# Delta-rule layer: the triangular inverse's blocks turned on chip by VectorE instead of through DRAM, with other fill rates

## The chip, the cores and the metric

One core of one Trainium2 chip runs the whole kernel. The time is the device time of one execution in microseconds (us). The core's engines are named as in the profile: PE (matmuls), PEld (its weight loads), DVE (VectorE), ACT (ScalarE), POOL (GpSimd), and SP, which issues most DMAs.

## The reference

The kernel computes one layer on 512 latent tokens of width 1024 with 256 context tokens: a half-step SwiGLU block, then a neighbourhood attention and a gated delta rule side by side, merged by sigmoid gates, then a second half-step SwiGLU block. The part that matters here is the gated delta rule. It has 4 heads of size 128 and runs in two directions over chunks of tokens. For each chunk with keys k, queries q, decays g and weights beta it needs

```
B  = strict_lower(k k^T) * beta * exp(g_i - g_j)     (a gram matrix with decay)
T  = (I + B)^-1                                      (unit lower triangular)
A  = lower(q k^T) * exp(g_i - g_j)
u  = T (beta (v - exp(g) k S));  out = exp(g) q S + A u;  S <- exp(g_last) S + k_tail^T u
```

(B is meant up to transposition; the kernel keeps Bt, At and Tt.) In parallel the projections of the attention and the gates, products of the modulated tokens with the matrix w_in, have to be made as well.

## The kernel before

The layer runs stage by stage: modulation vectors, the first SwiGLU block, the projections, the delta rule, attention, merge, the second SwiGLU block. Matmuls in full precision are made of three: each operand is split into a high part (ACT casts `wh`, L137) and the rest (DVE subtracts `wl`, L139), and `mm3k` issues hi·hi (L192), lo·hi (L193) and hi·lo (L194), 128x512 each.

**The delta rule** has 48 systems of 128x128: six chunk positions s, two pairs of heads p, and for each of these two directions by two heads. They go in three batches of two positions (bi 0, 1, 2; st 0, 1 inside a batch), 16 systems each; `gram(p, s, ...)` makes one group of four. It loads the decay differences by a DMA from `gcd` into Dt (for some positions into an accumulator buffer, `oacc`, that is still free), masks them with four VectorE steps (L1122), takes the exponential on ACT, gets k·kT from PE and multiplies it by beta and the decay into Bt (four steps, L1128). For later positions it also makes At (L1134) from q·kT. The masks of positions 2 and 3 are issued behind the last Bt of the first batch, those of 4 and 5 behind an At.

**The inverse.** Each 128x128 matrix is inverted by its 32x32 diagonal blocks first. A batch has 64 of them, and `base_inverse` (L1140) works on all at once: each block lies on two partitions of the 128, with 16 of its columns on each. To get that layout, `gram` writes Bt to a DRAM buffer `bd` (L1131), and four DMAs read the diagonal blocks back, two of them by way of `Ltr` and an ACT copy of 64x1024 (L1153). POOL clears the start Xt and writes ones and, into L, a diagonal of -1 (L1155). Then 31 rows follow, one multiplication (L1159) and one reduction (L1160) each on DVE. The result goes to a second DRAM buffer, `rd` (L1163), from which `inverse` (L1173) loads T0 and T1 in four DMAs (L1180), turns both by 32x32 blocks on DVE (L1182, L1183) and goes on with products of 32x32, then 64x64 blocks on PE (`pi`), with DVE and ACT between them. It ends with Tt, which the scan steps of the positions (`scan_step`, PE tiles `pc`) take.

**Fills.** Between these dependent steps PE makes the 28 projections of the list FILLS, each in four steps of six matmuls; ACT or DVE moves each finished one (`spill`) to DRAM. `turn(kind, i)` emits fill steps at rates by a table: "g" in the grams of each batch, "l" ahead of the first inverse, "i" after each product of an inverse of batch i, "s" in the scan steps. They are issued behind the last matmul of the delta rule by `issue_after`. Fill steps come in one sequence, so each follows the one before it. What is left, but for the last three projections, is emitted before the attention begins; its first matmul writes the scores, `sc` (L1446).

**Order.** The code runs grams of batch 0, grams of batch 1, the turn "l", inverse (0,0), four steps of base 1, inverse (0,1), then scans and grams of batch 2 mixed with the inverses of batch 1, then inverse (2,0), two scans, inverse (2,1) and the last scans. A scheduler at build time places the instructions of each engine in one fixed order, by readiness and by the `issue_after` marks.

Of the kernel before, what the change touches and what calls it, by code (L numbers as in the profile page):

```python
# [13 lines left out]
ALU = mybir.AluOpType  # L14
AX = mybir.AxisListType.X
# [3 lines left out]
P = 128  # L19
# [12 lines left out]
MSTR = P * P + P  # L32
# [26 lines left out]
def body(ctx, tc, I, out, dbg=None):  # L59
# [983 lines left out]
    RATE = {"g": (2, 3.0, 0.7), "l": (7.2,), "i": (1.5, 0, 0), "s": (0.7, 0.9, 0.5)}  # L1043
# [63 lines left out]
    def decay_place(s, p):  # L1107

        if s == 2 or s < 2 and p == 1:
            a = 2 * (s == 2)  # L1110
            return oaccs[p if s == 2 else s][:, a:a + 2].rearrange("p a b c -> p (a b) c")
        return tl(gb_, [P, 4, P], "Dt", 2)[:]

    def gram(p, s, bd, g):
# [4 lines left out]
        for m, (d, c, i) in enumerate(mats):  # L1119
            msk = cst[:, (C_MF if d == 0 else C_MB):][:, 0:P]  # L1120
            with tc.issue_after(marks["At" if s > 3 else "Bt"]) if s > 1 else nullcontext():
# [3 lines left out]
        for n, t in enumerate(products(p, s)):  # L1125
            if n == 0:
                for m, (d, c, i) in enumerate(mats):
                    b = V.scalar_tensor_tensor(Bt[:, m], t[m] if s == 1 else t[:, m], beta[:, d, s, 2 * p + i:2 * p + i + 1], Dt[:, m], op0=ALU.mult, op1=ALU.mult)  # L1128
                if s < 2:
                    marks["Bt"] = b.ins  # L1130
                nc.sync.dma_start(bass.AP(bd.tensor, bd.offset + g * MSTR, [[P, P], [4 * MSTR, 4], [1, P]]), Bt[:])  # L1131
# [8 lines left out]
    def base_inverse(bd, rd):  # L1140


        L = tl(gb_, [P, 32, 32], "L")
        tr = tl(gb_, [64, 32, 32], "Ltr")
        Xt = tl(gb_, [P, 16, 32], "Xt", 2)
        G.memset(Xt[:], 0.0)
        for q in range(4):
            G.memset(Xt[32 * q:32 * q + 32].rearrange("p c k -> p (c k)")[:, q % 2:512:34], 1.0)
        st = 32 * P + 32
        for q in range(4):  # L1150
            dst = tr[32 * q:32 * q + 32] if q < 2 else L[32 * q:32 * q + 32]
            nc.sync.dma_start(dst, bass.AP(bd.tensor, bd.offset + (q // 2) * 8 * MSTR, [[st, 32], [P, 32], [1, 32]]))
        S.copy(L[0:64].rearrange("p r c -> p c r"), tr[:])  # L1153

        G.memset(L[:].rearrange("p r c -> p (r c)")[:, 0:1024:33], -1.0)  # L1155
        for i in range(1, 32):
# [3 lines left out]
            V.tensor_reduce(Xt[:, 0:c, i], t[:, 0:c, 0:i + 1], AX, ALU.add, negate=True)  # L1160
            if i % 4 == 0:
                yield
        nc.sync.dma_start(bass.AP(rd.tensor, rd.offset, [[512, P], [1, 512]]), Xt[:].rearrange("p c k -> p (c k)"))  # L1163
# [9 lines left out]
    def inverse(bi, st, rd, Bts):  # L1173


# [742 lines left out]
```

## Time and profile before

| | us |
|---|---|
| three runs | 1496.15, 1498.07, 1498.37 (median 1498.07) |
| the profiled execution | 1495.44 |
| its span in the profile | 1493.7 |
| mean granted TensorE clock | 0.993 |
| delta-rule stage around the change | from about 740 to 967 of the span |

In the profile's rows a time is in microseconds from the start of the span; a group's row gives line, engine, operation, destination<-sources and shapes, then busy time, mean ns of one instruction, and the idle time of the engine just before them with what ended it. A row of the waits gives who waited, for what, the total us, how many times, and the longest. A row of a stretch gives its bounds, its length, the busy us and count of each engine, then the granted clock and the DMA share with GB/s.

### The profile page before, as it was taken

The numbers are of one execution on the slowest core, as the hardware profiler recorded it, in microseconds if no ns is written. First come the engines' busy times: TensorE is split into PE (matmuls) and PEld (weight loads), VectorE is DVE, ScalarE is ACT, GpSimd is POOL, SyncE is SP. The second block draws the span as 40 slices with busy tenths as digits, with TensorE's granted clock in tenths as the row PEclk, the third lists the DMA queues.
The fourth block names the chain that finished last, engine by engine and source line by source line (L and its number), as shares of the span: only waits on it lengthen the run. The fifth ranks groups of instructions, "written<-read, shape, count | busy, mean of one in ns | idle before, by whom it ended". The sixth has DMA issues, their size and how long they took to land.

```text
span 1493.7 us, 23926 instructions
## 1 busy us (share of the span) xinstructions
PE 1434.0 (96%) x9117; PEld 1258.3 (84%) x9117; DVE 1144.7 (77%) x1975; ACT 661.9 (44%) x1090; POOL 212.4 (14%) x262
## 2 busy tenths in 40 slices
PE   6999999999999999999998899999999999999997
PEld 4778989999998777888886778877778999998886
DVE  8787869999987565768787886666668799886627
ACT  5433524434333286545544434376526454444310
POOL 1000000000000121223301002243321022220001
PEclk9999999999999999999999999999999999999999
DMA  9676665454559554222577524274344143234732
GB/s 372 211 257 225 222 238 187 137 174 166 170 198 404 181 178 129 84 92 88 159 222 203 167 68 125 92 276 131 100 169 149 64 129 113 85 114 134 263 98 84
DMA packets 109236, 248.56 MB, mean 166 GB/s; under 512 B 29049, under 2 KB 44481, under 8 KB 109121
## 3 DMA queue, kind: packets, MB, share of 16 engines
q1 hardware_dynamic: 104480, 229.40, 46.6%
q0 software_dynamic: 3056, 12.33, 2.2%
q10 hardware_dynamic: 1586, 5.32, 0.9%
q8 instruction: 71, 1.16, 0.3%
q14 instruction: 43, 0.35, 0.1%
HBM read 215.50 MB, written 31.50 MB: 165 GB/s over the span
## 4 chain that ended last, share of the span: by engine, by line
PE 71%; DMA 10%; DVE 9%; ACT 4%; issue 3%; POOL 1%; SPq 1%; DVEq 0%; ACTq 0%; POOLq 0%
PE ps L211 15%; PE pm L192 5%; PE pm L193 5%; PE pm L194 5%; PE ps L533 4%; PE ps L535 4%; PE ps L534 4%; PE ps L1692 3%; PE ps L1694 3%; PE ps L1693 3%; PE ps L193 3%; PE ps L192 3%; PE ps L194 3%; PE pc L1049 3%; DMA wr<-in_up_dram 2%
## 5 line engine op out<-in xcount | busy, mean ns | idle before, releaser
L139 DVE TENSOR_TENSOR wl<-wr,wh 128x1024 fp32r<-128x1024 f32 (+1 forms) x184 | 226.0, 1233 | 112.9 <-ACT wh L137 111.3
L137 ACT CAST wh<-wr 128x1024 fp32r<-128x1024 f32 (+1 forms) x184 | 185.6, 1013 | 278.5 <-PE pm L193 72.7
L192 PE MATMUL pm<-uxh,wh 128*128 128x512 f32 x320 | 131.6, 411 | 0.0
L194 PE MATMUL pm<-uxh,wl 128*128 128x512 f32 x320 | 126.3, 395 | 0.8 <-DVE wl L139 0.8
L193 PE MATMUL pm<-uxl,wh 128*128 128x512 f32 x320 | 126.5, 395 | 0.0
L211 PE MATMUL ps<-wh,hx 128*128 128x512 f32 x352 | 96.1, 391 | 0.1
L211 PEld LDWEIGHTS ps<-wh,hx 128*128 128x128 f32 x352 | 65.9, 188 | 14.5 <-ACT wh L137 0.5
L280 DVE SCALAR_TENSOR_TENSOR adap<-wr,crow 128x1024 f32<-128x1024 f32 x61 | 74.3, 1218 | 2.4 <-DMA wr<-in_w_adaT_dram 1.7
L192 PE MATMUL ps<-uh,wh 128*128 128x256 f32 (+1 forms) x208 | 69.2, 334 | 3.8 <-ACT wh L137 3.8
L194 PEld LDWEIGHTS pm<-uxh,wl 128*128 128x128 f32 x320 | 60.6, 190 | 13.8 <-DVE wl L139 0.9
L192 PEld LDWEIGHTS pm<-uxh,wh 128*128 128x128 f32 x320 | 60.8, 190 | 11.1 <-ACT spill L796 0.2
L193 PEld LDWEIGHTS pm<-uxl,wh 128*128 128x128 f32 x320 | 60.9, 190 | 10.3
L114 POOL TENSOR_TENSOR rs<-ve,mhalf 128x1 f32<-128x1 f32 (+2 forms) x46 | 49.0, 1066 | 140.6 <-DVE ve L110 138.2
L193 PE MATMUL ps<-ul,wh 128*128 128x256 f32 (+1 forms) x208 | 67.9, 327 | 0.0
L194 PE MATMUL ps<-uh,wl 128*128 128x256 f32 (+1 forms) x208 | 67.0, 328 | 0.0
L193 PE MATMUL ps<-uxl,wh 128*128 128x256 f32 (+1 forms) x192 | 60.5, 318 | 2.2 <-DVE uxl L139 2.2
L192 PE MATMUL ps<-uxh,wh 128*128 128x256 f32 (+1 forms) x192 | 59.8, 318 | 1.6 <-ACT uxh L137 1.4
L194 PE MATMUL ps<-uxh,wl 128*128 128x256 f32 (+1 forms) x192 | 60.1, 316 | 0.0
L137 ACT CAST wh<-ra 128x1024 fp32r<-128x1024 f32 x31 | 32.6, 1052 | 59.7 <-PE ps L534 20.2
L533 PE MATMUL ps<-ur,wh 128*128 128x384 f32 x168 | 56.5, 336 | 0.0
L534 PE MATMUL ps<-ur,wh 128*128 128x384 f32 x168 | 56.4, 336 | 0.0
L533 PE MATMUL ps<-uh,wh 128*128 128x384 f32 x168 | 56.4, 336 | 0.0
(502 smaller groups left out, 4252.0 us busy)
## 6 DMA issues: line engine op xcount, KB each, us to landing
wr<-in_w_adaT_dram SPq DMA_DIRECT2D x64, 512.0 KB, 4.7
wr<-in_up_dram SPq DMA_DIRECT2D x56, 512.0 KB, 3.6
wr<-in_win_dram SPq DMA_DIRECT2D x52, 512.0 KB, 3.6
wr<-in_dn_dram SPq DMA_DIRECT2D x51, 512.0 KB, 4.1
ra<-in_up_dram SPq DMA_DIRECT2D x24, 512.0 KB, 4.3
rb<-in_up_dram SPq DMA_DIRECT2D x18, 512.0 KB, 4.0
ra<-in_w_adaT_dram SPq DMA_DIRECT2D x16, 512.0 KB, 5.0
wr<-in_w_o_dram SPq DMA_DIRECT2D x8, 512.0 KB, 4.4
```

The costliest lines, as they stand in the source:

```text
L114: G.tensor_tensor(rs[:], ve[:], mhalf[:, 0:n], ALU.pow)
L137: S.copy(hi, src)
L139: marks["lo"] = V.tensor_tensor(lo, src, hi.bitcast(F32), ALU.subtract).ins
L192: T.matmul(ps, a, uh[:, k, :], start=(k == 0), stop=False)
L193: T.matmul(ps, a, ul[:, k, :], start=False, stop=False)
L194: marks["mm"] = T.matmul(ps, b, uh[:, k, :], start=False, stop=(k == nk - 1)).ins
L211: T.matmul(banks[t][d][:, c0:c1], a[:, sl], b[:, d * 512 + c0:d * 512 + c1], start=first and j == 0, stop=last and j == 2)
L280: V.scalar_tensor_tensor(pr[:], raw[:], 1.0, crow, op0=ALU.mult, op1=ALU.mult, accum_out=col[:, c:c + 1])
L533: T.matmul(ps[:], a, mh, start=k == 0, stop=False)
L534: T.matmul(ps[:], a, ml, start=False, stop=False)
L535: T.matmul(ps[:], b, mh, start=False, stop=k == 3)
L1049: last[0] = T.matmul(*a, **k).ins
```

## The change

Both trips through DRAM are gone, and with them `bd`, `rd`, `Ltr` and POOL's memsets.

A new function `blocks` follows each Bt. Four ACT copies take the diagonal blocks of the two backward systems into D1 (32 partitions x 64 each), one DVE transpose of 32x32 blocks turns D1 into D2 (128x64), four ACT copies put those of the two forward systems straight into a buffer W (32 partitions, 128 elements with a stride), and one POOL copy puts D2 there. `base_inverse` turns W into L by one DVE transpose of 128x1024 and writes the diagonal by a DVE memset. The 31 rows are as before. Then a DVE transpose of 128x512 turns Xt into Z, four ACT copies take T0 and T1 out of Z, and the two transposes per position that were there before follow. Those four tiles go through the list `turned` to `inverse`. The start of Xt is now an input, `xt0`, loaded by one DMA. D1, D2, W and L have one buffer each; the next L is issued behind the Z before it. The decay of position 3 goes to a buffer "r" of another pool, and the masks of positions 2 and 3 are issued behind rows 3 and 9 of the base inverse, so no longer behind the last Bt.

In the rates, "g" of batch 1 goes from 3.0 to 2.5 and "l" from 7.2 to 2; "i" of batch 2 goes from 0 to 0.5 and "s" of batch 2 from 0.5 to 0.9. The 39 fill steps ahead of the first inverse become 30.

```diff
     spool, done = [gq], [0]
     gb_, close_gb = pool("gbase", "right")
     FS, N0, NKQ, NLATE = 4, 2, 2, 3
-    RATE = {"g": (2, 3.0, 0.7), "l": (7.2,), "i": (1.5, 0, 0), "s": (0.7, 0.9, 0.5)}
+    RATE = {"g": (2, 2.5, 0.7), "l": (2,), "i": (1.5, 0, 0.5), "s": (0.7, 0.9, 0.9)}
     NBT, NAT, NT6, NTT = 8, 8, 1, 2
     last = [None]
...
         if s == 2 or s < 2 and p == 1:
             a = 2 * (s == 2)
             return oaccs[p if s == 2 else s][:, a:a + 2].rearrange("p a b c -> p (a b) c")
+        if s == 3:
+            return tl(gq, [P, 4, P], "r", 2)[:]
         return tl(gb_, [P, 4, P], "Dt", 2)[:]
-    def gram(p, s, bd, g):
+    def blocks(W, Bt, p, st):
+        D1 = tl(gb_, [P, 2, 32], "D1")
+        for b in range(4):
+            r = slice(32 * b, 32 * b + 32)
+            S.copy(D1[r], Bt[r, 2:4, r])
+        D2 = tl(gb_, [P, 2, 32], "D2")
+        V.transpose(D2[:].rearrange("p m c -> p (m c)"), D1[:].rearrange("p m c -> p (m c)"))
+        w = W[:].rearrange("p c q m -> p m c q")
+        m0 = 8 * st + p
+        for b in range(4):
+            r = slice(32 * b, 32 * b + 32)
+            S.copy(w[r, m0:m0 + 3:2], Bt[r, 0:2, r][:, :, :, None].to_broadcast([32, 2, 32, 2]))
+        G.tensor_copy(w[:, m0 + 4:m0 + 7:2], D2[:, :, :, None].to_broadcast([P, 2, 32, 2]))
+    def gram(p, s, W):
         mats = mats_of(s)
         Dt = decay_place(s, p)
         nc.sync.dma_start(Dt[:], bass.AP(gcd.tensor, gcd.offset + (4 * s + 2 * p) * P, [[0, P], [24 * P, 2], [1, 2 * P]]))
         for m, (d, c, i) in enumerate(mats):
             msk = cst[:, (C_MF if d == 0 else C_MB):][:, 0:P]
-            with tc.issue_after(marks["At" if s > 3 else "Bt"]) if s > 1 else nullcontext():
+            with tc.issue_after(marks["At" if s > 3 else ("row", 3 if s == 2 else 9)]) if s > 1 else nullcontext():
                 V.scalar_tensor_tensor(Dt[:, m], Dt[:, m], gcum[:, d, s, 2 * p + i:2 * p + i + 1], msk, op0=ALU.subtract, op1=ALU.add)
         S.activation(Dt[:], Dt[:], AF.Exp)
         Bt, At = tl(gq, [P, 4, P], "Bt", NBT), None
         for n, t in enumerate(products(p, s)):
             if n == 0:
                 for m, (d, c, i) in enumerate(mats):
-                    b = V.scalar_tensor_tensor(Bt[:, m], t[m] if s == 1 else t[:, m], beta[:, d, s, 2 * p + i:2 * p + i + 1], Dt[:, m], op0=ALU.mult, op1=ALU.mult)
-                if s < 2:
-                    marks["Bt"] = b.ins
-                nc.sync.dma_start(bass.AP(bd.tensor, bd.offset + g * MSTR, [[P, P], [4 * MSTR, 4], [1, P]]), Bt[:])
+                    V.scalar_tensor_tensor(Bt[:, m], t[m] if s == 1 else t[:, m], beta[:, d, s, 2 * p + i:2 * p + i + 1], Dt[:, m], op0=ALU.mult, op1=ALU.mult)
+                blocks(W, Bt, p, s % 2)
             else:
                 At = tl(gq, [P, 4, P], "At", NAT)
                 a = V.tensor_tensor(At[:], t[:], Dt[:], ALU.mult)
...
         return Bt, At
-    def base_inverse(bd, rd):
+    turned = []
+    def base_inverse(W, Xt):
         L = tl(gb_, [P, 32, 32], "L")
-        tr = tl(gb_, [64, 32, 32], "Ltr")
-        Xt = tl(gb_, [P, 16, 32], "Xt", 2)
-        G.memset(Xt[:], 0.0)
-        for q in range(4):
-            G.memset(Xt[32 * q:32 * q + 32].rearrange("p c k -> p (c k)")[:, q % 2:512:34], 1.0)
-        st = 32 * P + 32
-        for q in range(4):
-            dst = tr[32 * q:32 * q + 32] if q < 2 else L[32 * q:32 * q + 32]
-            nc.sync.dma_start(dst, bass.AP(bd.tensor, bd.offset + (q // 2) * 8 * MSTR, [[st, 32], [P, 32], [1, 32]]))
-        S.copy(L[0:64].rearrange("p r c -> p c r"), tr[:])
-        G.memset(L[:].rearrange("p r c -> p (r c)")[:, 0:1024:33], -1.0)
+        with tc.issue_after(marks["Z"]) if "Z" in marks else nullcontext():
+            V.transpose(L[:].rearrange("p r c -> p (r c)"), W[:].rearrange("p c q m -> p (c q m)"))
+        V.memset(L[:].rearrange("p r c -> p (r c)")[:, 0:1024:33], -1.0)
         for i in range(1, 32):
             c = (i + 1) // 2
             t = tl(gb_, [P, 16, 32], "bt")
             V.tensor_tensor(t[:, 0:c, 0:i + 1], L[:, i:i + 1, 0:i + 1].to_broadcast([P, c, i + 1]), Xt[:, 0:c, 0:i + 1], ALU.mult)
-            V.tensor_reduce(Xt[:, 0:c, i], t[:, 0:c, 0:i + 1], AX, ALU.add, negate=True)
+            marks[("row", i)] = V.tensor_reduce(Xt[:, 0:c, i], t[:, 0:c, 0:i + 1], AX, ALU.add, negate=True).ins
             if i % 4 == 0:
                 yield
-        nc.sync.dma_start(bass.AP(rd.tensor, rd.offset, [[512, P], [1, 512]]), Xt[:].rearrange("p c k -> p (c k)"))
+        Z = tl(gb_, [P, 16, 32], "bt")
+        marks["Z"] = V.transpose(Z[:].rearrange("p c k -> p (c k)"), Xt[:].rearrange("p c k -> p (c k)")).ins
+        z = Z[:].rearrange("p c (q m) -> p m (c q)", q=2)
+        fl = lambda t, m: t[:, m:m + 4].rearrange("p m c -> p (m c)")
+        for st in range(2):
+            T0 = tl(gq, [P, 8, 32], "T0", 2)
+            T1 = tl(gq, [P, 8, 32], "T1", 2)
+            S.copy(T0[:, 0:4], z[:, 8 * st:8 * st + 4])
+            S.copy(T1[:, 4:8], z[:, 8 * st + 4:8 * st + 8])
+            V.transpose(fl(T1, 0), fl(T0, 0))
+            V.transpose(fl(T0, 4), fl(T1, 4))
+            turned.append((T0, T1))
         yield
...
         G.memset(t[:], 0.0)
     inv_n = [0]
-    def inverse(bi, st, rd, Bts):
-        T0 = tl(gq, [P, 8, 32], "T0", 2)
-        T1 = tl(gq, [P, 8, 32], "T1", 2)
-        for dst, d in ((T1, 0), (T0, 1)):
-            for q in range(2):
-                nc.sync.dma_start(dst[q:P:2, 4 * d:4 * d + 4], bass.AP(rd.tensor, rd.offset + (2 * d + q) * 16384 + st * 2048, [[32, 64], [2 * 2048, 4], [1, 32]]))
-        fl = lambda t, m: t[:, m:m + 4].rearrange("p m c -> p (m c)")
-        V.transpose(fl(T0, 0), fl(T1, 0))
-        V.transpose(fl(T1, 4), fl(T0, 4))
+    def inverse(bi, st, Bts):
+        T0, T1 = turned.pop(0)
         blk = [slice(32 * b, 32 * b + 32) for b in range(4)]
...
             nc.sync.dma_start(obd[2 * p + i], o)
     Sst = [None, None]
-    res, rds, inv = {}, {}, {}
+    res, inv = {}, {}
     def grams(bi):
-        bd = tl(dp, [16 * MSTR], f"bd{bi}")[:]
-        rds[bi] = tl(dp, [64, 1024], f"rd{bi}")[:]
+        W = tl(gb_, [P, 32, 2, 16], "W")
+        Xt = tl(gb_, [P, 16, 32], "Xt", 2)
+        nc.sync.dma_start(Xt[:].rearrange("p c k -> p (c k)"), I["xt0"])
         for j in (0, 2, 1, 3) if bi == 0 else range(4):
-            res[(bi, j)] = gram(j % 2, 2 * bi + j // 2, bd, 2 * (j % 2) + j // 2)
-        return base_inverse(bd, rds[bi])
+            res[(bi, j)] = gram(j % 2, 2 * bi + j // 2, W)
+        return base_inverse(W, Xt)
     def step(gen, n=8):
         for _ in range(n):
             next(gen, None)
     def inv_of(bi, st):
-        inv[(bi, 2 * st)], inv[(bi, 2 * st + 1)] = inverse(bi, st, rds[bi], [res[(bi, 2 * st + p)][0] for p in range(2)])
+        inv[(bi, 2 * st)], inv[(bi, 2 * st + 1)] = inverse(bi, st, [res[(bi, 2 * st + p)][0] for p in range(2)])
     def scan_of(bi, j):
         p = j % 2
...
     return c
+def _start():
+    t = np.zeros((P, 16, 32), np.float32)
+    for q in range(2):
+        for c in range(16):
+            t[np.arange(P) % 32 // 16 == q, c, 2 * c + q] = 1.0
+    return t.reshape(P, 512)
 def _rope():
     f = (10000.0 ** (-np.arange(32, dtype=np.float32) / np.float32(32))).astype(np.float32)
     t = np.arange(NX)
...
     a = {}
     a["ident"] = np.eye(P, dtype=np.float32)
     a["cst"] = _consts()
+    a["xt0"] = _start()
     a["rope"] = _rope()
     a["x"] = g["x"][0]
     a["ctx"] = g["ctx"][0]```

Three places in the order of the instructions carry the rest. The first is on DVE, ahead of the first base inverse. `Bt` is a gram with decay, `oacc` and `Dt` hold the decays that the masks (L1122) work on, `wl` is a split for a fill, and the first row with `bt` starts the base inverse. Before:

```order
L1128 SCALAR_TENSOR_TENSOR Bt_7059<-pq_7043,beta_5207,oacc_1279_6940 128x128 x4
L1122 SCALAR_TENSOR_TENSOR oacc_1278_6939<-oacc_1278_6939,gcum_5208,cst_5205 128x128 x4
L1122 SCALAR_TENSOR_TENSOR oacc_1279_6940<-oacc_1279_6940,gcum_5208,cst_5205 128x128 x4
L1122 SCALAR_TENSOR_TENSOR Dt_7405<-Dt_7405,gcum_5208,cst_5205 128x128 x4
L139 TENSOR_TENSOR wl_7102<-wr_7099,wh_7101 128x1024
L1122 SCALAR_TENSOR_TENSOR Dt_7489<-Dt_7489,gcum_5208,cst_5205 128x128 x4
L139 TENSOR_TENSOR wl_7266<-wr_7263,wh_7265 128x1024
L1159 TENSOR_TENSOR bt_7147<-L_7133,Xt_7135 128x2
```

The same place on DVE now (`D<-D` is D2 from D1, `L<-W` the large transpose):

```order
L1144 SCALAR_TENSOR_TENSOR Bt_7093<-pq_7066,beta_5207,oacc_1279_6940 128x128 x4
L1122 STREAM_TRANSPOSE D_1293_7028<-D_1292_7023 128x64
L138 TENSOR_TENSOR wl_7147<-wr_7144,wh_7146 128x1024
L1122 STREAM_TRANSPOSE D_1297_7052<-D_1296_7047 128x64
L1122 STREAM_TRANSPOSE D_1301_7080<-D_1300_7075 128x64
L1122 STREAM_TRANSPOSE D_1304_7103<-D_1303_7098 128x64
L1160 STREAM_TRANSPOSE L_7178<-W_7003 128x1024
L138 TENSOR_TENSOR wl_7325<-wr_7322,wh_7324 128x1024
L1161 MEMSET L_7178 128x32
L1165 TENSOR_TENSOR bt_7181<-L_7178,Xt_7004 128x2
```

The sixteen mask steps between the last Bt and the first row of the base inverse have moved behind it, and five transposes stand in their place.

The second place is on DVE too, a few rows further, inside the base inverse, now (`bt` and `Xt` are its rows; the `oacc` steps at L1138 are masks of position 2):

```order
L1166 TENSOR_REDUCE Xt_7004<-bt_7187 128x2
L1138 SCALAR_TENSOR_TENSOR oacc_1278_6939<-oacc_1278_6939,gcum_5208,cst_5205 128x128 x3
L1165 TENSOR_TENSOR bt_7190<-L_7178,Xt_7004 128x2x5
L1138 SCALAR_TENSOR_TENSOR oacc_1278_6939<-oacc_1278_6939,gcum_5208,cst_5205 128x128
L1138 SCALAR_TENSOR_TENSOR oacc_1279_6940<-oacc_1279_6940,gcum_5208,cst_5205 128x128 x4
L1166 TENSOR_REDUCE Xt_7004<-bt_7190 128x2
L1144 SCALAR_TENSOR_TENSOR Bt_7297<-pq_7298,beta_5207,oacc_1278_6939 128x128 x4
L1148 TENSOR_TENSOR At_7349<-pq_7341,oacc_1278_6939 128x512
```

Before, no mask of position 2 stands between these rows: they are those shown ahead of the base inverse.

The third place is on PE, at the first product (`pi<-T,Bt`) of inverse (2,0). `pm` are fills, `pc` scan steps. Before:

```order
L194 MATMUL pm_9053<-uxh_4690,wl_8980 128x512
L1049 MATMUL pc_9083<-vn_9076,ktail_9078 128x128 x4
L1049 MATMUL pc_9093<-S_1619_8724,qT_5227 128x128
L1049 MATMUL pc_9093<-S_1619_8724,qT_5228 128x128
L192 MATMUL pm_9053<-uxh_4690,wh_8979 128x512
L1049 MATMUL pi_8870<-T_1632_8854,Bt_8139 32x32 x4
L1049 MATMUL pi_8870<-T_1632_8854,Bt_8166 32x32 x4
L193 MATMUL pm_9053<-uxl_4691,wh_8979 128x512
L194 MATMUL pm_9053<-uxh_4690,wl_8980 128x512
```

The same place on PE now:

```order
L193 MATMUL pm_8776<-uxh_4690,wl_8630 128x512
L1048 MATMUL pc_9008<-S_1596_8617,kT_5221 128x128
L1048 MATMUL pc_9018<-r_9013,Tt_1277_6935 128x128 x4
L1048 MATMUL pc_9036<-vn_9029,ktail_9031 128x128 x4
L1048 MATMUL pc_9052<-S_1596_8617,qT_5225 128x128
L1048 MATMUL pc_9068<-vn_9029,At_7515 128x128 x4
L1048 MATMUL pc_9088<-S_1632_8760,kT_5223 128x128
L1048 MATMUL pi_8897<-T_1612_8678,Bt_8128 32x32 x4
L1048 MATMUL pi_8897<-T_1612_8678,Bt_8182 32x32 x4
L191 MATMUL pm_8776<-uxh_4690,wh_8629 128x512
L192 MATMUL pm_8776<-uxl_4691,wh_8629 128x512
```

(Of rows that repeat, one is shown.) Before, 493 of the 600 fill matmuls of the stage stand ahead of this product, and fills lie between the scan steps; now 396 stand ahead, none of them between the last scan steps, and the rest is behind the product.

More of the change, by code (lines that the diff above doesn't have):

```diff
@@ L31 @@
 BWD_CH = (1, 0, 5, 4, 3, 2)
-MSTR = P * P + P
 C_MF = 0
```

## Prediction

> **What bounds the kernel now.** I read the page's totals, then the waits of TensorE (PE) over the delta-rule stage, then VectorE's (DVE) waits and the busy time by stretch, then the timelines at the places where one waits for the other.
>
> ```profile
> span 1493.7 us, 23926 instructions
> PE 1434.0 (96%) x9117; PEld 1258.3 (84%) x9117; DVE 1144.7 (77%) x1975; ACT 661.9 (44%) x1090; POOL 212.4 (14%) x262
> ```
>
> PE is busy for 96% of the span, so the time can fall only where PE waits. The stage around the change runs from the last strip of the first gram blocks to the first attention scores; its waits:
>
> ```profile
> PE pi L1049 <- DVE Y L1229: 5.1, 3, 2.4
> PE pi L1049 <- DMA T<-rd: 4.3, 1, 4.3
> PE pc L1049 <- DVE bt L1159: 1.8, 1, 1.8
> PE pi L1049 <- DVE T L1218: 1.6, 2, 1.0
> PE pc L1052 <- DVE oacc L1315: 1.1, 1, 1.1
> PE pc L1049 <- ACT Tt L1237: 0.9, 2, 0.5
> PE pq L1049 <- DVE Xt L1160: 0.9, 1, 0.9
> PE pm L194 <- DVE wl L139: 0.8, 1, 0.8
> PE pc L1049 <- DVE r L1260: 0.7, 2, 0.4
> ```
>
> (Columns: total us, times, longest.) Together 17.2 us; only one row, 4.3 us, is the trip through DRAM. Nothing in this stage can gain more than 17.2. The rest is DVE being late, and DVE in turn waits:
>
> ```profile
> 756.00:802.20 46.20, 41.01 (x205) 34.15 (x204) 39.21 (x111) 17.71 (x24) 1.16 (x6) 1.00 0.80 239
> 802.20:913.20 111.00, 102.90 (x1002) 85.52 (x1001) 89.81 (x250) 46.43 (x103) 12.68 (x23) 0.97 0.45 138
> 913.20:967.00 53.80, 50.51 (x536) 43.16 (x534) 31.30 (x69) 18.43 (x42) 14.52 (x22) 1.00 0.23 76
> ```
>
> Each row gives the length, then the busy us of PE, weight load, DVE, ACT and POOL. The cuts are: first base row, first inverse, first inverse of batch 2, scores. DVE's waits in the middle stretch:
>
> ```profile
> DVE T L1182 <- DMA T<-rd: 3.5, 4, 1.7
> DVE Dt L1122 <- DMA Dt<-gcd: 3.1, 1, 3.1
> DVE r L1260 <- PE pc L1049: 2.5, 2, 1.5
> DVE vn L1269 <- PE pc L1049: 2.1, 3, 1.2
> DVE oacc L1297 <- PE pc L1049: 2.0, 2, 1.6
> DVE T L1183 <- DMA T<-rd: 1.6, 1, 1.6
> DVE bt L1159 <- POOL L L1155: 1.4, 1, 1.4
> ```
>
> In that stretch DVE is busy 89.8 of 111.0 us. So DVE's chain sets when each inverse can start, and fills (the projection matmuls that PE does between) cover most of what PE would otherwise wait. Both have to be followed: when T of batch 2 is ready, and what PE still has to do then.
>
> **Part 1: the way into the first base inverse.**
>
> ```profile
> 741.48 2.15 DVE L1128 SCALAR_TENSOR_TENSOR Bt<-pq,beta,oacc 128x128 f32<-128x128 f32 x8
> ...
> 747.55 1.22 DVE L139 TENSOR_TENSOR wl<-wr,wh 128x1024 fp32r<-128x1024 f32 x1
> 748.69 1.13 DVE L1122 SCALAR_TENSOR_TENSOR Dt<-Dt,gcum,cst 128x128 f32<-128x128 f32 x4
> 755.99 0.16 DVE L1159 TENSOR_TENSOR bt<-L,Xt 128x2 f32<-128x2 f32 x1 [5.03 <-POOL L L1155]
> ```
>
> That is DVE's timeline (start, us, the last with its wait); the groups that price the new operations (busy, mean ns) are:
>
> ```profile
> L1153 ACT COPY L<-Ltr 64x1024 f32<-64x1024 f32 x3 | 6.3, 2111 | 3.3 <-DMA Ltr<-bd 3.3
> L1193 ACT COPY T<-T 32x256 f32<-32x256 f32 x24 | 9.7, 402 | 8.3 <-issue 4.3 <-DVE T L1182 3.2 <-DMA T<-rd 0.6
> L1219 ACT ACTIVATE Tt<-pi 32x128 f32<-32x128 f32 x24 | 6.4, 268 | 4.8 <-PE pi L1049 4.5
> L137 ACT CAST wh<-wr 128x1024 fp32r<-128x1024 f32 x28 | 29.3, 1045 | 68.2 <-PE pm L193 55.1 <-issue 11.8 <-DMA wr<-in_win_dram 1.2
> L798 ACT ACTIVATE spill<-pm 128x512 f32<-128x512 f32 x16 | 9.4, 589 | 0.0
> L1194 POOL COPY Tt<-T 32x256 f32<-32x256 f32 x24 | 10.5, 439 | 19.6 <-PE pc L1049 8.0 <-DVE Xt L1160 3.7 <-DVE T L1183 3.1
> L1182 DVE STREAM_TRANSPOSE T<-T 128x128 f32<-128x128 f32 x6 | 1.8, 303 | 3.5 <-DMA T<-rd 3.5
> ```
>
> Before, the last two grams' Bt are made from 741.48 to 743.63 (8 pieces), 1.05 a gram, so the first of the four is ready at about 740.5. Base 0 starts at 755.99, 12.4 us after the last Bt, for the DRAM trip, the copy and the memset. After, ACT takes 16 copies into W and 16 into D1, with one cast (1.05) and one spill (0.59) among them in its order. A W copy writes 128 elements with a stride. Its bounds are 0.27 (L1219: 128 elements, written in a row) and 0.53 (that plus 128 x 2.06 ns, L1153's whole time by its 1,024 elements, the one row with scattered writes); I take 0.40, half-way. A D1 copy reads 64 elements: at most 0.27, taken 0.25, at least nothing. So ACT needs 6.4 + 4.0 + 1.6 = 12.0 us from 740.5: 752.5. Behind it come the last D2 transpose (0.2, at most the 0.30 of L1182), the POOL copy (0.44) and the transpose of W into L (between 0.3, L1182, and 1.22, the 128x1024 row of L139; taken 1.1, as it has L139's columns), then a wl split or the small memset: base 0 starts at about **755**, bounds 751 and 758. One DRAM trip has been changed for a chain of small copies of the same length.
>
> [...]
>
> **Part 2: to the first inverse.** The ends of the old chain, on DVE and PE:
>
> ```profile
> 790.12 0.69 DVE L1160 TENSOR_REDUCE Xt<-bt 128x16 f32<-128x512 f32 x1
> ...
> 802.00 0.92 PE L1049 MATMUL pi<-T,Bt 32*32 32x32 f32 x32 [4.33 <-DMA T<-rd]
> 913.49 0.45 PE L1049 MATMUL pi<-T,Bt 32*32 32x32 f32 x32
> 966.99 0.39 PE L1446 MATMUL sc<-kah,qah 64*128 64x256 f32 x2
> ```
>
> Base 0 took 34.8 us (755.99 to 790.81), DVE busy nearly throughout. The masks of the second batch now stand inside it: they used to fill the wait of part 1, which is gone as cover. 20 more masks at 0.28 (1.13 for 4) are 5.6, four D2 transposes 0.8, one At 0.6: about 41.8. Then Z (0.6, between 0.30 and 0.69), L of the next batch (1.1, ACT's 0.4 copies beside it) and the two T transposes (0.5): PE's first inverse at 755 + 44 = **799** against 802.0. The 11 us from 790.81 to 802.00 have shrunk to 2.2, but 7 of the 9 went to masks that had been hidden.
>
> **Part 3: to the first inverse of batch 2.** DVE's 89.8 us get L, two Z and four D2 (+3.1), some base rows that used to run ahead of 802 (+2.0), and lose two wl splits (2.4) and one scan part's r and vn, which move behind (an estimate of 1.8: four of 128x128 at the mask's 0.28, one of 128x512 at L1160's 0.69): 91. Of its 21.2 us of idle time the rows T (3.5, 1.6) and L (1.4) go; of the waits for PE (6.6 in the rows) I leave half, as fewer fills stand ahead; the mask's 3.1 and small gaps stay: about 10. So 101 us instead of 111.5: T of batch 2 is on PE at **900** against 913.5, 13.5 earlier. Bounds: 888 (base at 751, 2 us of idle) and 908 (base at 758, 15 idle).
>
> **Part 4: what PE still has to do then.** The order has 97 fewer fill matmuls ahead of that inverse (396 against 493) and the same 600 ahead of the scores. What a fill costs, from PE's timeline:
>
> ```profile
> 768.04 1.05 PE L1049 MATMUL pq<-kT 128*128 128x128 f32 x8
> 768.85 0.48 PE L192 MATMUL pm<-uxh,wh 128*128 128x512 f32 x1
> ...
> 773.03 0.27 PE L1049 MATMUL pq<-qT,kT 128*128 128x128 f32 x1
> ```
>
> The 18 fills from 768.85 to 773.03 are 0.232 us each, so 97 are 22.5. They stand behind the inverse in PE's order, so PE cannot do them while it waits for T. Three groups of 8 scan matmuls (0.81 each, the 768.04 row to the next) are behind it too: 2.4. Of the last stretch's own waits (3.3 idle of 53.8) 2.5 get covered by the extra fills. The scores start at 900 + 53.5 + 22.5 + 2.4 - 2.5 = 975.9 against 967.0: **+9 us**. In PE's terms: it comes to the first inverse 12.5 us of fills (54 matmuls) sooner while T comes 3 us sooner, so that it waits some 9 us more there, and the rest of the stage wins nothing back. After the scores the order is the same.
>
> The profiled execution took 1495.44 (1.74 beyond its span), 2.6 below the median of the runs shown, 1498.07. The sum gives 1495.44 + 9 = 1504.4 there; against the median **1507**.
>
> **Rivals.** *A, the waits go and nothing replaces them (faster).* For it: DVE idles 11.5 us for L and T in the rows above (5.0, 1.4, 3.5, 1.6), and ACT has over half of its time free in each stretch. If the copies overlap with the Bt products and are at their lower bounds, base 0 starts at 751; with the long transposes near L1182's 0.30 parts 2 and 3 shrink to 43 and 89, and with 2 us of idle time left T of batch 2 is there at 885. The point that decides is 891: 891 + 75.9 = 967. At 885 the scores come 6 us sooner: **1492**. Against it: the masks lost their cover, and DVE's waits for PE and gcd have nothing to do with the layout.
>
> *B, no difference.* T of batch 2 between 888 and 894: the removed waits pay just for the fills that moved, **1495 to 1501**.
>
> [...]
>
> *D, the change does not do what it says:* the turns on chip leave base 0 where it was (755 against 756 is already my forecast), and only the rates act. That is my part 2 with part 3 as before: 799 + 111.5, T at 910.5, +19: **1517**.
>
> **Chances.** Forecast (1501 to 1511): 0.44. A: 0.26. B: 0.14. C and D: 0.16. A measurement of this kernel can tell about 0.2% (3 us) from no change, so faster 0.26, same 0.14, slower 0.60. The range reaches from just below A's time, 1491, to just beyond C's, 1515, and leaves D and the edges out; the forecast's own range is 1501 to 1511.
>
> **What would show it.** Right: base 0 starts at 753 to 757; PE waits 8 us or more at the first inverse for a DVE transpose instead of a DMA; pi of batch 2 at 897 to 904; then a long run of fills without waits; scores at 973 to 979; POOL's copies near 0.44. Wrong: base 0 before 752, pi of batch 2 before 891, or PE waits in the stage below 17 us in all, which would make the sum of parts 3 and 4 false.

## The result, and the profile after

The changed kernel takes **1517.8 us** (median of four runs, 1517.61 to 1521.5) against 1498.22 for the kernel before (four runs, 1496.15 to 1499.74): the ratio is 1.0137, 95% interval 1.0118 to 1.0157. It is slower, as forecast, but by 20 us and not by 9, and outside the range named (1491 to 1515). The profiled execution took 1517.96 and fits the median. The totals of the page:

```profile
span 1516.0 us, 23937 instructions
PE 1441.0 (95%) x9117; PEld 1262.7 (83%) x9117; DVE 1155.3 (76%) x1996; ACT 691.6 (46%) x1195; POOL 214.1 (14%) x256
```

The same 9117 matmuls are busy for 7 us longer than before (1434.0), and PE stands still for 15 us more. PE's six longest of nine waits from the first gram product (736.5) to the scores (988.4):

```profile
PE pi L1048 <- DVE T L1179: 13.7, 2, 13.3
PE pc L1048 <- DVE vn L1278: 3.6, 3, 1.6
PE pi L1048 <- DVE Y L1238: 3.4, 2, 2.3
PE pq L1048 <- DVE Bt L1144: 3.2, 1, 3.2
PE pm L191 <- ACT spill L795: 2.6, 1, 2.6
PE pc L1048 <- DVE S L1293: 2.0, 2, 1.1
```

The wait for a DMA at the first inverse has become a wait for a DVE transpose, and from 4.3 us it has grown to 13.3. Two waits are new: for the Bt of a later gram (3.2), and for a spill on ACT (2.6). Now the stretches of the stage, cut in both kernels at the first gram product, the first inverse, the first inverse of batch 2 and the scores (length, then busy us of PE, weight load, DVE, ACT, POOL, then the granted clock, the DMA share and GB/s). Before:

```profile
733.20:802.00 68.80, 62.86 (x316) 52.69 (x315) 53.04 (x153) 28.53 (x39) 1.31 (x7) 1.00 0.80 235
802.00:913.50 111.50, 103.40 (x1004) 85.68 (x1005) 90.31 (x251) 46.70 (x104) 12.94 (x24) 0.97 0.46 138
913.50:967.00 53.50, 50.21 (x534) 43.11 (x533) 31.00 (x68) 18.16 (x41) 14.26 (x21) 1.00 0.23 76
```

After:

```profile
736.50:808.10 71.60, 52.44 (x264) 43.64 (x262) 54.01 (x154) 43.09 (x102) 3.58 (x9) 0.92 0.49 165
808.10:910.10 102.00, 91.87 (x937) 75.33 (x937) 90.63 (x260) 50.26 (x128) 8.33 (x21) 0.96 0.26 91
910.10:988.40 78.30, 75.77 (x654) 64.17 (x654) 38.29 (x79) 28.82 (x60) 20.91 (x27) 1.00 0.31 107
```

The stage has grown from 233.8 to 251.9 us, by 18.1. PE's busy time in it went from 216.5 to 220.1, its idle time (length less busy) from 17.3 to 31.8. The first stretch idles 19.2 us instead of 5.9, the middle one 10.1 instead of 8.1. The last is longer because 120 more matmuls stand in it. The other 4.2 us of the difference between the spans lie outside the stage: 3.3 ahead of it, where the instructions of both kernels are the same (the first gram product starts at 733.2 in the kernel before, and between 733.8 and 738.3 in the kernels below), and 0.9 behind it.

DVE's timeline at the first base inverse:

```profile
744.97 2.15 DVE L1144 SCALAR_TENSOR_TENSOR Bt<-pq,beta,oacc 128x128 f32<-128x128 f32 x8
747.03 0.23 DVE L1122 STREAM_TRANSPOSE D<-D 128x64 f32<-128x64 f32 x1
752.34 1.23 DVE L138 TENSOR_TENSOR wl<-wr,wh 128x1024 fp32r<-128x1024 f32 x1 [5.07 <-ACT wh L136]
753.79 0.25 DVE L1122 STREAM_TRANSPOSE D<-D 128x64 f32<-128x64 f32 x1 [0.23 <-ACT D L1120]
755.18 0.24 DVE L1122 STREAM_TRANSPOSE D<-D 128x64 f32<-128x64 f32 x1 [1.14 <-ACT D L1120]
756.57 0.25 DVE L1122 STREAM_TRANSPOSE D<-D 128x64 f32<-128x64 f32 x1 [1.14 <-ACT D L1120]
757.32 1.25 DVE L1160 STREAM_TRANSPOSE L<-W 128x1024 f32<-128x1024 f32 x1 [0.51 <-POOL W L1128]
758.49 1.18 DVE L138 TENSOR_TENSOR wl<-wr,wh 128x1024 fp32r<-128x1024 f32 x1
759.66 0.09 DVE L1161 MEMSET L<- 128x32 f32 x1
759.78 0.16 DVE L1165 TENSOR_TENSOR bt<-L,Xt 128x2 f32<-128x2 f32 x1
```

And ACT's, of the same time:

```profile
743.53 1.68 ACT L1127 COPY W<-Bt 32x128 f32<-32x128 f32 x4 [1.02 <-DVE Bt L1144]
745.22 1.00 ACT L1120 COPY D<-Bt 32x64 f32<-32x64 f32 x4
746.25 4.98 ACT L1127 COPY W<-Bt 32x128 f32<-32x128 f32 x12
751.26 1.04 ACT L136 CAST wh<-wr 128x1024 fp32r<-128x1024 f32 x1
752.21 0.58 ACT L795 COPY spill<-pm 128x512 f32<-128x512 f32 x1
752.69 1.00 ACT L1120 COPY D<-Bt 32x64 f32<-32x64 f32 x4
754.07 1.01 ACT L1120 COPY D<-Bt 32x64 f32<-32x64 f32 x4 [0.38 <-DVE D L1122]
755.46 1.00 ACT L1120 COPY D<-Bt 32x64 f32<-32x64 f32 x4 [0.38 <-DVE D L1122]
```

From the last Bt (747.1) to the first row of the base inverse are 12.7 us, against 12.4 by way of DRAM. ACT's twelve W copies stand ahead of a cast and of the spill that PE waited 2.6 us for, and the last D copies go in turns with DVE, because D1 is one buffer.

### The profile page after: what moved, and what is told of

Read it like the earlier page. It is cut to its first block, busy times and chain, and to the rows that moved or that the text cites. A ratio compares the mean times of both kernels' runs of the same rounds, so it can differ in the third digit from the quotient of the medians.

```text
span 1516.0 us, 23937 instructions
## 1 busy us (share of the span) xinstructions
PE 1441.0 (95%) x9117; PEld 1262.7 (83%) x9117; DVE 1155.3 (76%) x1996; ACT 691.6 (46%) x1195; POOL 214.1 (14%) x256
## 4 chain that ended last, share of the span: by engine, by line
PE 72%; DVE 11%; DMA 7%; ACT 5%; issue 4%; POOL 1%; SPq 0%; DVEq 0%; ACTq 0%; POOLq 0%
PE ps L210 15%; PE pm L191 5%; PE pm L192 5%; PE pm L193 5%; PE ps L532 4%; PE ps L534 4%; PE ps L533 4%; PE ps L1702 3%; PE ps L1704 3%; PE ps L1703 3%; PE ps L191 3%; PE ps L192 3%; PE ps L193 3%; PE pc L1048 2%; DVE wl L138 1%
## 5 line engine op out<-in xcount | busy, mean ns | idle before, releaser
L138 DVE TENSOR_TENSOR wl<-wr,wh 128x1024 fp32r<-128x1024 f32 (+1 forms) x184 | 225.7, 1232 | 132.4 <-ACT wh L136 131.8
L136 ACT CAST wh<-wr 128x1024 fp32r<-128x1024 f32 (+1 forms) x184 | 185.6, 1013 | 254.9 <-PE pm L192 60.8
L191 PE MATMUL pm<-uxh,wh 128*128 128x512 f32 x320 | 133.1, 416 | 2.6 <-ACT spill L795 2.6
L193 PE MATMUL pm<-uxh,wl 128*128 128x512 f32 x320 | 127.4, 398 | 0.0
L192 PE MATMUL pm<-uxl,wh 128*128 128x512 f32 x320 | 127.1, 397 | 0.0
L210 PEld LDWEIGHTS ps<-wh,hx 128*128 128x128 f32 x352 | 65.8, 188 | 15.9 <-ACT wh L136 2.0
L191 PEld LDWEIGHTS pm<-uxh,wh 128*128 128x128 f32 x320 | 61.5, 192 | 14.3 <-ACT spill L795 3.0
L191 PE MATMUL ps<-uh,wh 128*128 128x256 f32 (+1 forms) x208 | 68.9, 332 | 4.2 <-ACT wh L136 4.2
L193 PEld LDWEIGHTS pm<-uxh,wl 128*128 128x128 f32 x320 | 61.1, 191 | 13.6 <-DVE wl L138 0.5
L192 PEld LDWEIGHTS pm<-uxl,wh 128*128 128x128 f32 x320 | 61.6, 192 | 10.5
L192 PE MATMUL ps<-ul,wh 128*128 128x256 f32 (+1 forms) x208 | 67.6, 326 | 0.0
L193 PE MATMUL ps<-uh,wl 128*128 128x256 f32 (+1 forms) x208 | 66.8, 327 | 0.0
L192 PE MATMUL ps<-uxl,wh 128*128 128x256 f32 (+1 forms) x192 | 61.2, 321 | 2.2 <-DVE uxl L138 2.2
L191 PE MATMUL ps<-uxh,wh 128*128 128x256 f32 (+1 forms) x192 | 60.5, 322 | 1.6 <-ACT uxh L136 1.4
L193 PE MATMUL ps<-uxh,wl 128*128 128x256 f32 (+1 forms) x192 | 60.7, 319 | 0.0
L136 ACT CAST wh<-ra 128x1024 fp32r<-128x1024 f32 x31 | 32.6, 1052 | 59.5 <-PE ps L533 20.2
L533 PE MATMUL ps<-ur,wh 128*128 128x384 f32 x168 | 56.4, 336 | 0.0
L532 PE MATMUL ps<-uh,wh 128*128 128x384 f32 x168 | 56.4, 336 | 0.0
```

The costliest lines, as they stand in the source:

```text
L136: S.copy(hi, src)
L138: marks["lo"] = V.tensor_tensor(lo, src, hi.bitcast(F32), ALU.subtract).ins
L191: T.matmul(ps, a, uh[:, k, :], start=(k == 0), stop=False)
L192: T.matmul(ps, a, ul[:, k, :], start=False, stop=False)
L193: marks["mm"] = T.matmul(ps, b, uh[:, k, :], start=False, stop=(k == nk - 1)).ins
L210: T.matmul(banks[t][d][:, c0:c1], a[:, sl], b[:, d * 512 + c0:d * 512 + c1], start=first and j == 0, stop=last and j == 2)
```

## The experiments

Two theories. **Rates**: most of the loss is the new order of the fills, and the turn on chip is about neutral. **Turn**: the chain of small copies and the masks inside base 0 make T late, and with it everything behind. A third question is the clock. In the table T1 is the first inverse and T2 the first inverse of batch 2; lengths, and idle as length less PE's busy time, come from the stretches, fills are those of the stage. The intervals are those of the ratio to the kernel before, run beside them (medians 1498.22 to 1499.65). Lengths come from one profiled execution of each kernel, which can lie some us from the median (new rates alone: 1521.77 against 1517.38; masks early: 1509.45 against 1514.14). What comes behind the scores, to the end of the span, varies between 525 and 533 us from kernel to kernel (537 in one), since each build orders the later stages a little differently; the stage is therefore read apart from the total.

```
kernel                    median   ratio (95%)              to T1  T1-T2  T2-scores  stage  idle  fills ahead of T1, T1-T2, behind
before                    -        1                         68.8  111.5   53.5      233.8  17.3  234 259 107
changed                   1517.80  1.0137 (1.0118-1.0157)    71.6  102.0   78.3      251.9  31.8  180 216 204
turn, old rates           1503.75  1.0024 (1.0013-1.0035)    73.6  104.6   55.7      233.9  15.9  234 252 114
new rates alone           1517.38  1.0116 (1.0094-1.0138)    68.8  104.3   80.3      253.4  30.6  180 216 204
masks early               1514.14  1.0089 (1.0069-1.0109)    68.1   98.0   80.7      246.8  27.4  180 216 204
no D1                     1514.32  1.0103 (1.0082-1.0124)    67.5  105.7   74.9      248.1  27.9  180 216 204
wait filled               1525.36  1.0168 (1.0146-1.0189)    70.7  103.7   75.0      249.4  20.1  180 216 204 (and 54 idle ones)
front rates               1514.59  1.0113 (1.0090-1.0136)    74.5  104.9   74.4      253.8  23.8  234 216 174
catch-up                  1527.22  1.0187 (1.0164-1.0210)    71.3  122.3   68.6      262.2  33.0  180 349  95
no D1, early, old rates   1501.65  1.0019 (1.0005-1.0032)    70.4  105.3   59.2      234.9  14.8  234 245 121
the same, half on POOL    1503.90  1.0041 (1.0025-1.0057)    69.1  107.6   60.0      236.7  15.2  234 245 121
before, more ahead        1501.93  1.0016 (1.0003-1.0029)    68.4  112.7   53.6      234.7  15.7  234 275  91
turn, early, more ahead   1499.71  0.9994 (0.9979-1.0009)    71.9  106.0   56.4      234.3  15.0  234 269  97
```

**Each half of the change alone.** The turn with the old table:

```diff
-    RATE = {"g": (2, 2.5, 0.7), "l": (2,), "i": (1.5, 0, 0.5), "s": (0.7, 0.9, 0.9)}
+    RATE = {"g": (2, 3.0, 0.7), "l": (7.2,), "i": (1.5, 0, 0), "s": (0.7, 0.9, 0.5)}
```

> The changed kernel with the old table of rates. Theory 'rates' (most of the loss is fills that no longer stand ahead of T): the 54 fills that come back (12.5 us) fit into the 13.3 us for which PE waits at the first inverse, that wait falls below 3 us, and the time is 1500 to 1505. Theory 'turn' (the chain of small copies and the masks inside base 0 make T late, and everything behind it): the time stays above 1511, with base 0 longer still, since two more wl splits and four more casts and spills stand in it.

The kernel before with the new table (the same lines the other way):

> The kernel before with the new table of rates alone. Theory 'rates': PE comes to the first inverse 12.5 us sooner while T comes at most 2.5 us sooner, so it waits 13 to 15 us there for the load of T, and the 97 fills behind the inverse of batch 2 lengthen the end: 1511 to 1518. Theory 'turn': at most 1504.

The turn alone costs 0.24%, 3.6 us; the rates alone cost 1.16%, 17 us, nearly the whole of the change. In the stage the turn with the old rates costs nothing (233.9 us against 233.8), and the new rates cost 19.6. At the first inverse, with the turn and the old rates:

```profile
PE pi L1048 <- DVE T L1179: 5.3, 1, 5.3
```

and with the old layout and the new rates:

```profile
PE pi L1049 <- DMA T<-rd: 18.2, 2, 16.1
```

The second kernel has both DRAM trips and none of the new copies, and it waits 16.1 us there: it lacks 54 fills ahead of a T that comes no sooner (68.8 us after the first gram product, as before). "Rates" holds, "turn" falls as the main cause. The wait with the turn and the old rates was 5.3, not below 3: T comes 4.8 us later than before.

**Where the turn loses its time.** The masks of positions 2 and 3 go back behind the last Bt:

```diff
-            with tc.issue_after(marks["At" if s > 3 else ("row", 3 if s == 2 else 9)]) if s > 1 else nullcontext():
+            with tc.issue_after(marks["At" if s > 3 else "Bt"]) if s > 1 else nullcontext():
...
+                if s < 2:
+                    marks["Bt"] = b.ins
```

> The changed kernel with the masks of positions 2 and 3 issued behind the last Bt again, where DVE waits for ACT's copies. Theory 'turn': 16 masks at 0.27 leave base 0, it gets some 4 us shorter, T is there 4 us sooner, and the time is 1511 to 1514. Theory 'rates' as well, as long as PE waits at the first inverse; if the masks collide with the copies there (DVE has a wl and four D2 in that stretch) the gain is below 2 us: 1516 to 1518.

Base 0 got 6.4 us shorter (39.6 against 46.0) but started 2.8 later (26.1 us after the first gram product against 23.3), since the sixteen masks, four Bt steps and an At now stand ahead of it. DVE's idle time there fell from 11.2 to 7.8 us, and T came 3.5 sooner; 1514.14 lies at the upper edge of the range named. Taking D1 away instead (D2 gets a second buffer with it):

```diff
-        D1 = tl(gb_, [P, 2, 32], "D1")
+        D2 = tl(gb_, [P, 2, 32], "D2", 2)
...
-            S.copy(D1[r], Bt[r, 2:4, r])
-        D2 = tl(gb_, [P, 2, 32], "D2")
-        V.transpose(D2[:].rearrange("p m c -> p (m c)"), D1[:].rearrange("p m c -> p (m c)"))
+            V.transpose(D2[r], Bt[r, 2:4, r])
```

> The changed kernel without D1: DVE turns the backward blocks straight out of Bt, four transposes of 32x64 a gram instead of four ACT copies and one transpose of 128x64. Theory 'rates': ACT's queue ahead of base 0 loses 4 us of copies and the three turns of waiting for D2 (1.1 us each), the waits of DVE for D1 inside base 0 (3.0) go, T comes 5 to 7 us sooner, PE's wait at the first inverse falls from 13.3 to 7 to 9, and the time is 1511 to 1514, still far above before, because the fills still stand behind. Theory 'turn': with the chain of small copies broken, most of the loss goes: below 1507.

Base 0 started 4.0 us sooner (19.3), as ACT's copies left; T came 4.1 sooner, not 5 to 7. Inside base 0 DVE no longer waits for D, but base 0 is as long as it was (45.9): sixteen transposes take 3.8 us there, where four took 1.0, and one more wl split takes 1.2. The wait at the first inverse did not get shorter (13.5), as PE got there sooner too. The time, 1514.32, lies just above the range of "rates" and far from that of "turn": by the medians either repair is worth some 3.5 us, in the stage 5.1 (masks) and 3.8 (no D1), and most of the loss stays.

**Is the wait itself the cost, or its effect on the clock?** The wait filled with matmuls that nobody reads:

```diff
+    idle = tl(pm, [P, NX], *PMB)
+    with tc.issue_after(last[0]):
+        for n in range(54):
+            T.matmul(idle[:], uxh[:, n % 8, 0:P], uxh[:, n % 8, :], start=True, stop=True)
     inv_of(0, 0)
```

> The changed kernel with 54 matmuls more, of 128x512 into a tile that nobody reads, ahead of the first inverse, where PE waits 13.3 us; they take 12.3 us. No work of the layer is moved. If the idle time alone is the cost, the time stays at 1516 to 1519. If PE's lower granted clock after the wait (0.50 and 0.83 in the two stretches of 10 us behind it) costs as well, the matmuls up to the inverse of batch 2, 91.9 us busy against some 87.8 at the price of before, get faster by 3 to 5 us: 1512 to 1515.

Its total, 1525.36, lies outside both ranges and says nothing of this: the stage is 2.5 us shorter, but from the scores to the end it takes 537.2 us against 527.6. Of these 9.6 us PE idles 4.7 and is busy 4.9 longer; waits for DVE's `sn` in the second SwiGLU block (3.7 us), which the changed kernel does not have, are in the idle part, and the rest is not explained. In the stage the clock can be read. Four stretches of 10 us around the first inverse, changed kernel:

```profile
790.00:800.00 10.00, 4.76 (x21) 3.59 (x20) 8.69 (x21) 2.83 (x5) 0.55 (x1) 0.99 0.65 213
800.00:810.00 10.00, 1.92 (x35) 1.66 (x36) 9.48 (x24) 2.94 (x8) 1.82 (x5) 0.50 0.10 26
810.00:820.00 10.00, 10.00 (x110) 7.25 (x110) 8.67 (x34) 4.21 (x10) 1.36 (x4) 0.83 0.25 81
820.00:830.00 10.00, 9.19 (x116) 6.93 (x115) 7.38 (x23) 8.17 (x22) 0.81 (x2) 1.00 0.55 169
```

With the wait filled:

```profile
790.00:800.00 10.00, 10.00 (x46) 8.28 (x45) 8.82 (x22) 4.19 (x10) 0.55 (x1) 1.00 0.67 223
800.00:810.00 10.00, 9.48 (x73) 7.56 (x72) 9.56 (x22) 2.40 (x7) 1.05 (x3) 1.00 0.13 40
810.00:820.00 10.00, 10.00 (x121) 7.32 (x121) 9.10 (x38) 6.13 (x16) 2.11 (x6) 1.00 0.27 88
820.00:830.00 10.00, 9.20 (x146) 6.91 (x143) 5.89 (x18) 6.80 (x18) 0.81 (x2) 1.00 0.74 196
```

The clock after the wait (third figure from the end) is 0.50 and 0.83 in the first kernel and 1.00 in the second. Cut at the right places, the clock of the changed kernel is 0.50 from PE's restart at 808.10 to 813.40 and 1.00 from there to 820.00, so about 2.7 us of PE's work were lost (an estimate: half of 5.3). With the wait filled PE is busy for 217 us in the stage without the extra matmuls (12.2), 3 us less than in the changed kernel, and the stage is 2.5 us shorter. T2 came no sooner after T1 (103.7 us against 102.0), but the build also put 24 more scan matmuls ahead of T2 here (2.4 us), and PE idled longer there (12.0 us against 10.1). So the lower clock is shown; its price is 2.5 to 3 us at most, and the runs do not separate it from the changed order.

**Which place of the fills counts?** Old rates up to the first inverse only:

```diff
-    RATE = {"g": (2, 2.5, 0.7), "l": (2,), "i": (1.5, 0, 0.5), "s": (0.7, 0.9, 0.9)}
+    RATE = {"g": (2, 3.0, 0.7), "l": (7.2,), "i": (1.5, 0, 0.5), "s": (0.7, 0.9, 0.9)}
```

> The changed kernel with the old rates up to the first inverse (54 fills back ahead of it) and the new ones behind it; 450 fills stand ahead of the inverse of batch 2 (396 with the change, 493 before), and one projection more, 24 fills, ahead of the scores, which is then missing behind them. If the wait at the first inverse is the loss, 11 to 13 us of the 18 come back: 1503 to 1508. If the fills behind the inverse of batch 2 are, at most half does: 1509 to 1514.

And low rates there with high ones between the two inverses:

```diff
+    RATE = {"g": (2, 2.5, 0.7), "l": (2,), "i": (2.2, 0.4, 0), "s": (1.2, 1.4, 0.5)}
```

> The changed kernel with its low rates up to the first inverse (180 fills ahead of it), but high ones between that and the inverse of batch 2: 529 fills ahead of the latter (396 with the change, 493 before), 95 behind it, and 24 more ahead of the scores. Theory 'order behind the inverse of batch 2' (what stands behind it is paid in full, what stands ahead is free): the last stretch falls from 78 to 53 us and the time to 1497 to 1502. Theory 'idle time' (PE's work is the same, so only its idle time counts, and the 13 us at the first inverse cannot be won back later): the 10 us of idle time between the two inverses fill up, the wait at the first inverse stays, and the time is 1504 to 1510.

The first repaired the wait at the first inverse (5.6 us) and yet stayed at 1514.59, just above the second of its ranges: T2 came as late as ever (104.9 behind T1 with 216 fills, and 104.6 with 252 in the kernel with all the old rates), and the 174 fills behind it were paid there. Of its stage 5.6 us are the 24 fills more. The second went the other way and was worst of all, 1527.22, outside both expectations. Its fills between the inverses did fill that idle time (3.5 us left), but they stood between dependent steps and pushed T2 from 102.0 to 122.3; other delta-rule work slid behind it (488 matmuls that are no fills, 448 in the changed kernel), and PE idles 10.2 us there instead of 2.5. The longest waits of the stage, the first of them at the first inverse and the second behind T2:

```profile
PE pi L1048 <- DVE T L1179: 14.3, 1, 14.3
PE pc L1051 <- DVE oacc L1324: 7.0, 4, 3.0
PE pc L1048 <- DVE vn L1278: 4.5, 3, 3.5
```

So neither "what stands ahead of T2 is free" nor "only the sum of idle time counts, and the middle can take it" is right by itself. The two runs fit a narrower rule: a fill is free only where PE would otherwise wait at that very point.

**Can the turn win?** With no D1, early masks and the old rates; the same with the W copies of two of the four blocks on POOL:

```diff
-            S.copy(w[r, m0:m0 + 3:2], Bt[r, 0:2, r][:, :, :, None].to_broadcast([32, 2, 32, 2]))
+            (S.copy if b < 2 else G.tensor_copy)(w[r, m0:m0 + 3:2], Bt[r, 0:2, r][:, :, :, None].to_broadcast([32, 2, 32, 2]))
```

> Without D1, the masks of positions 2 and 3 behind the last Bt, and the old rates. Theory 'rates': T of the first inverse comes some 64 us after the first gram product (68.8 before, 73.6 with the turn and the old rates), PE's wait there goes, and the time is 1494 to 1500, the kernel before or up to 0.3% better. Theory 'turn': masks and transposes only change places on DVE, T stays at 70 or more, and the time is 1500 to 1504.

> As the kernel without D1, with early masks and old rates, and half of the copies into W on POOL instead of ACT (8 of 16 a batch). If ACT's queue still sets the start of base 0, it comes 3 us sooner; with no wait left at the first inverse this is worth nothing in time (within 2 us of that kernel). If POOL's copies and DVE's base rows hinder each other, base 0 gets longer by 2 us or more and the time 2 to 5 us higher.

Both miss the better expectation: 1501.65 and 1503.90. What was expected under "turn" for the first came true: masks and transposes only change places on DVE. T came at 70.4 and 69.1, not 64. In the first DVE is busy for 62.7 of the 70.4 us ahead of T (54.0 of 71.6 in the changed kernel): 24 more transposes take 5.5 us and the two wl splits of the returned fills 2.6. Copies on POOL shortened base 0 by 2.2 us and did not start it sooner. Last, more fills ahead of T2 and fewer behind, for the kernel before and for the turn with early masks:

```diff
+    RATE = {"g": (2, 3.0, 0.7), "l": (7.2,), "i": (1.5, 0, 0), "s": (0.9, 1.1, 0.2)}
```

> The kernel before with 16 more fills ahead of the inverse of batch 2 (509 of 600). PE idles 8.1 us between the two inverses, and 16 fills take 3.7. Both theories: the last stretch gets 3.7 us shorter; if DVE's chain alone sets when T of batch 2 is ready the time is 2 to 4 us below before; if the wl split that comes with them delays that chain (1.2 us), or PE is bound by its other matmuls there, it is within 1.5 us of before.

> The turn on chip with the masks behind the last Bt, the old rates up to the first inverse, and 503 fills ahead of the inverse of batch 2. If the turn has a gain at all, it must show here, with the order of the fills and the masks repaired: T of batch 2 some 5 us sooner than with the kernel before (175 us after the first gram product against 180) and the time 1494 to 1498. If the two DRAM trips were only exchanged for as much work on ACT and DVE: 1498 to 1503.

The first is no gain (1.0016) and lies outside both ranges: T2 moved back by 1.2 us, and the last stretch did not shrink though it holds 16 fills fewer (3.7 us). But the build also moved 32 scan matmuls behind T2 (456 matmuls there are no fills, 424 before), some 3.2 us at 0.81 for eight, so this run does not test the fills by themselves. The second is the best version with the turn, equal to the kernel before: 0.9994, interval 0.9979 to 1.0009. Its T2 came 177.9 us after the first gram product, not 175 (180.3 before), and the time is in the range for an even exchange. None of the kernels beat the kernel before.

## Why the prediction was wrong

The direction and the mechanism were right: PE comes to the first inverse 54 fills sooner while T does not come that much sooner, and what was taken from there is paid behind the inverse of batch 2. The new rates alone show it. Two forecasts came out closely. The middle stretch took 102.0 us (forecast 101, before 111.5), and the first base inverse began no sooner: 23.3 us after the first gram product (forecast 21.8, before 22.8), 16 W copies at 0.41 us and 16 D1 copies at 0.25 (medians; forecast 0.40 and 0.25) having replaced the DRAM trip.

**The step that failed is part 2**: "PE's first inverse at 755 + 44 = 799 against 802.0". From the first gram product it came after 71.6 us and not 65.8 (before 68.8): it got later, not sooner. Of the 5.8 us, 1.5 are the start and 4.2 base 0, 46.0 us long and not 41.8. DVE's waits inside it:

```profile
DVE D L1122 <- ACT D L1120: 3.0, 3, 1.3
DVE At L1148 <- DMA kq<-kqd: 1.1, 1, 1.1
DVE wl L138 <- ACT wh L136: 0.9, 2, 0.6
```

Together they are 5.0 us, where the base 0 of before has no wait behind its first row; DVE was busy for 39.6 us in it (33.2 before), 0.6 less than the sum implies, as one wl split fewer (1.2) stands there. The sum had counted only DVE's busy time, as if nothing it needs could be late. But the D2 transposes of the second batch stand in DVE's order between the base rows, and each waits for four ACT copies that queue behind W copies and casts; what stands behind it on DVE waits as well. Part 1 had seen ACT's queue ahead of base 0, part 2 forgot it inside. This is read from the changed kernel's trace; the two repairs do not prove it. Masks early gained its 3.5 us at T by filling idle time ahead of base 0, and without D1 the waits for D went but more transposes took their place. What base 0 takes with the same work and no waits, no run shows.

**Mis-sized terms.** Part 4 let the extra fills cover 2.5 us of the last stretch's waits; they covered 0.8, the stretch took 78.3 and not 75.9. No term stood for matmuls that get slower: PE was busy 3.6 us longer in the stage, and with the wait filled 3 us of that were gone. In the changed kernel's trace the granted clock is 0.50 for 5.3 us behind the 13.3 us wait. The prediction lengthened that wait and did not ask what follows from it. Part 3's own idle terms add up to 11.4 us (21.2 less 6.5 and 3.3); it took 10, and 11.4 were measured, which is its miss of 1.0. By stretches, 5.8 + 1.0 + 2.4 were missing, 9.2 us, which with the 9 forecast make the stage's 18.1.

**The rivals.** A fell: base 0 did not start at 751, and T2 was not there by 891; B fell with it. C had put the time at 1514. Its first ground, that POOL's copies and DVE's base rows hold each other up, was an assumption of the author's, and for DVE's side no run shows it: POOL's 12 copies took 0.41 us in the median and 0.44 on average (forecast 0.44), three of them 0.45 to 0.56 where they lay partly beside an `At` product of DVE, while the base rows took 21.1 us of DVE's time against 21.3 before, and with half of the W copies on POOL DVE's 528 instructions of the stage took 192.3 us against 193.2 with those copies on ACT. Its second ground, the turns of ACT, DVE and POOL with single buffers, was right in kind (the D2 transposes waited 6.9 us for ACT's copies into D1, ACT 0.8 us for the transposes), though C put their cost ahead of base 0 and in part 3, and it was paid inside base 0, the failed step above. D described the result best: the turn leaves the first inverse about where it was, and mainly the rates act. Its 1517 was that sum with the middle stretch unchanged, which did not happen; that it lies so near the measured 1517.8 is luck.

The range was too narrow at the top: part 2 had no bound for waits inside base 0, part 4 none for slower matmuls, and D, which came nearest, was left outside it.

## What to carry to other kernels

Where filler work hides a wait, the filler's table belongs to the length of that wait: new rates that reckon with an earlier result cost what they were to gain if the result isn't earlier (17 of 20 us here). A round trip through DRAM that is covered by other work can be traded for copies on engines only where these have free places at that point (here the turn alone cost 0.24%); count for each moved instruction what stands ahead of it in its engine's queue, also inside the chain, and not its duration alone. When many steps are moved, time each part alone: here the half that looked like a detail was the result.

## What the runs showed of the hardware

- A 32x32-block transpose on DVE took (medians of the changed kernel) 0.246 us for 128x64, 0.702 for 128x512 and 1.203 for 128x1024, about 1 ns a column and 0.2 us besides (an estimate from these three).
- An ACT copy of 32x128 with scattered writes took 0.408 us, one of 32x64 0.242 (medians of the changed kernel, 48 of each).
- After 13.3 us of waiting TensorE's granted clock was 0.50 for 5.3 us (808.10 to 813.40) and 1.00 in the 6.6 us after; with the wait filled it was 1.00 in each of the four stretches from 790 to 830.
- A POOL copy of 128x128 (the changed kernel's 12 into W) took 0.40 us with DVE at rest (at 747.33), 0.40 to 0.41 in nine cases in all, and 0.45, 0.55 and 0.56 in the three that lay partly beside an `At` product of DVE (128x512). These products took 0.68 to 0.69 us, as the others around them. Without D1 POOL's nine instructions from the first gram product to the first inverse took 4.55 us in all, against 3.58 in the changed kernel.
